# Moving the keys' turn behind the diagonal blocks, and two waits in steps of the weave, in a gated-delta decoder layer

## The chip, the cores and the metric

The kernel runs on one core of a Trainium2 chip. The metric is the device time of one execution in microseconds (us). The kernel before took 2161.29 us, the median of 3 runs between 2160.62 and 2162.14. Engines are TensorE (PE, matmuls), VectorE (DVE), ScalarE (ACT), GpSimd (POOL) and SyncE (SP); the last two, and ScalarE in a few places, also issue DMAs.

## The reference

One layer of a hybrid decoder, for one new sequence of 512 tokens and 8 sequences of one new token each (520 token columns), model width 2048, all in float32:

```python
h = h + W_out [ GatedDeltaNet(x_n) ; MultiScalePool(x_n) ],  where x_n = RMSNorm(h)
h = h + SwiGLU(RMSNorm(h))
```

One projection gives q, k, v, an output gate z, two gate logits and the pooling channels. q, k and v pass a causal convolution of 4 taps and SiLU. The delta group has 8 heads of width 128. Within a chunk of tokens a head solves a unit lower triangular system A U = V with A = I + (the strictly lower part of K K^T, scaled by beta and the decay), and between chunks it carries a 128 x 128 state:

```python
a_mat = m + jnp.eye(CHUNK, dtype=m.dtype)
u = lax.linalg.triangular_solve(a_mat, vc * bc[..., None], left_side=True,
                                lower=True, unit_diagonal=True)
...
v_new = u_i - jnp.einsum('bhck,bhkv->bhcv', w_i, S)
S = S * jnp.exp(g_last)[..., None, None] + jnp.einsum('bhck,bhcv->bhkv', k_dec, v_new)
```

The outputs are the two results of the layer, the final states, and the last rows for the convolution and the pooling.

## The kernel before, in words

**Products.** Each projection of 128 output columns (`product`) is 96 matmuls, 16 blocks of the inner dimension times two halves of the 520 columns times three: weights and activations are split into a high and a low part, and high x high, high x low and low x high are summed (lines 168 to 170, tile `mm`). The two halves hold a PSUM bank each, of three for all products, and are read out by VectorE (L259, `mixa<-mm` for the gate tiles z, `ext<-mm` for q, k and v); the product after next cannot start in a bank before that.

**The weave.** The small work of the heads is written as Python generators that lie between the matmuls of the products. After each 6 matmuls of a product `weave.step()` is called once; a step advances the first task of each of two tracks. A task that says `yield n` goes on n steps later, and `weave.add(task, track, delay)` starts one at least `delay` steps after the call. TensorE executes in the order in which the program was written, so a step count fixes where in the stream of matmuls a head's own matmuls (tile `dn`) stand. The other engines' streams are ordered by the framework's scheduler, which also goes by the order of the program, by what each instruction waits for and by its estimate of times; each of these streams then executes in that fixed order.

**Heads 0 to 3, then 4 to 7.** For each batch of four heads the products run k0 to k3, z0 to z3, then v and q of each head in turn. What the change touches:

- `turn_blocks` (L756 on) turns a 128 x 512 tile by 32 x 32 blocks. VectorE transposes into `bt` (L761 for keys and outputs, L766 for q and v), POOL stores that to memory (`tok_d`, L763 or L768) and loads it back with four DMAs (L771). For the keys the result is `kd`.
- `keys(h)` (L791 on, on track 1, 16 steps after its k product): the Gram matrix of the keys on TensorE (L795), its diagonal (L799, L801), a power -1/2 on POOL (L215, `rr`), scales `sck` (L805 to L808), the masked and scaled matrix (L810), then SyncE stores the 32 x 32 diagonal blocks (`nd_d`, L816) and POOL sets them to zero (L819).
- `eliminate(b)` (L823 on, track 1): SyncE loads the diagonal blocks of four heads (`nb<-nd_d`, L825). VectorE inverts all of them together by 31 pairs of instructions (L835, L837, tile `u`), copies the result transposed (L840, `ut`), and SyncE stores both (`ud_d`, L838 and L841).
- `qv_tiles(h)` (L1115 on): SyncE loads the inverted blocks into `utf` (L1117, four DMAs), the v product, v's taps (L737, L739, tile `y`), SiLU on ScalarE, v's turn into `vs`, then the same for q (`qT`, turned into `qk`); then `delta(h)` is added to track 0.
- `delta(h)` (L845 on): `xt_` from a product with the inverted blocks (L859), then the solution steps of a loop over `it` = 0, 1, 2 (matmul L869 into PSUM, VectorE L871 writes `uu`), each of which uses the `uu` of the step before, but the first. kd is scaled in step 0 (L874), vs in step 1 (L754). Then come four chunks, with the state `S` (L909, L911), and a tail that normalises the output (L931 to L936, a power on POOL among it) and turns it.

Loads of weights (`raw`, L131) stand on SyncE's queue among these DMAs; each is split into `hi` by ScalarE and `lo` by VectorE (L137).

Of the kernel before, what the change touches and what calls it, by code (L numbers as in the profile page):

```python
# [17 lines left out]
P = 128  # L18
# [3 lines left out]
SEQ = 512  # L22
# [47 lines left out]
def decoder_kernel(ctx, tc, x_prompt, x_sample, state_delta, state_conv, state_pool, norm_mix, w_in,  # L70
# [50 lines left out]
    weave = Weave()  # L121
# [399 lines left out]
    with ExitStack() as p1:  # L521
# [268 lines left out]
        def keys(h):  # L790
            kT, nn = mixb[:, h % 4, 0:SEQ], mixb[:, 4 + h % 4, 0:SEQ]  # L791
            _, dm = decay(h)
            gp_ = pst()
            for c in range(NCH):
                te.matmul(gp_[:, ck(c)], kT[:, ck(c)], kT[:, ck(c)], start=True, stop=True)  # L795
            ss = d1tile("ss", [P, NCH], "ss")
            junk = d1tile("junk", [P, P], "junk")
            for c in range(NCH):
                dve.scalar_tensor_tensor(junk, gp_[:, ck(c)], 1.0, ident, op0=ALU.mult, op1=ALU.mult,  # L799
                                         accum_out=ss[:, c:c + 1])  # L800
            dve.tensor_scalar(ss, ss, EPS, None, op0=ALU.add)  # L801
            rr = d1tile("rr", [P, NCH], "rr")
            pow_mhalf(rr, ss)
            fk, ik, ad = sck[:, h, 0, :], sck[:, h, 1, :], sck[:, h, 2, :]
            dve.tensor_tensor(fk, rr, rr, op=ALU.mult)  # L805
            dve.tensor_tensor(fk, fk, btok[:, 0:4, h], op=ALU.mult)
            dve.tensor_tensor(ik, ss, rr, op=ALU.mult)
            dve.tensor_tensor(ad, fk, edec[:, :, h], op=ALU.mult)  # L808
            for c in range(NCH):
                dve.scalar_tensor_tensor(nn[:, ck(c)], gp_[:, ck(c)], fk[:, c:c + 1], dm[:, ck(c)],  # L810
                                         op0=ALU.mult, op1=ALU.mult)
            yield 6 if h < 3 else 2
            nn3 = v3(nn)
            for q in range(4):
                r = slice(32 * q, 32 * q + 32)
                sp.dma_start(nd_d[h, q].rearrange("c s j -> s c j"), nn3[r, :, r])  # L816
            for q in range(4):
                r = slice(32 * q, 32 * q + 32)
                pool.memset(nn3[r, :, r], 0.0)  # L819


        def eliminate(b):
# [2 lines left out]
            sp.dma_start(nb.rearrange("p s j -> p (s j)"), nd_d[hs].rearrange("h q c s j -> (h q c) (s j)"))  # L825
            u = d1tile("u", [64, 32, 32], "u")
            uf = u.rearrange("p s j -> p (s j)")
            yield 10
            pool.memset(uf, 0.0)
            pool.memset(uf[:, 0:1024:33], 1.0)  # L830
            for t in range(31, 0, -1):
# [13 lines left out]
        def delta(h, qT, qk, vs):  # L845
# [19 lines left out]
            for it in range(3):  # L865
# [16 lines left out]
                                                 op0=ALU.mult, op1=ALU.mult)  # L882
                if it == 1:
                    scaled(vs, ik)
                yield 2

            op_ = pst()
            S = None
# [224 lines left out]
        def qv_tiles(h):  # L1113
            utf = utfs[h % 2].rearrange("p a c j -> p (a c) j")
            for q in range(4):  # L1115
                r = slice(32 * q, 32 * q + 32)
                sp.dma_start(utf[r, :, r], ud_d[h, q].rearrange("a c s j -> s (a c) j"))  # L1117
            vs = d1tile("vs", [P, SEQ], "vs")
            qkv_tile(2, h, vs)
            turn_blocks(2, h, vs, vs)  # L1120
            qT = d1tile("s0", [P, SEQ], "qT")
            qkv_tile(0, h, qT)
            qk = d1tile("tq", [P, SEQ], "qk")
            turn_blocks(0, h, qT, qk)
            weave.add(delta(h, qT, qk, vs), 0, 1)

        kds = {}
        for b in range(2):
            for h in range(4 * b, 4 * b + 4):
                qkv_tile(1, h, mixb[:, h % 4, 0:SEQ],  # L1130
                         {0: ext_first, 1: ext_second}.get(h))
                if h == 0:
                    weave.add(states())
                    weave.add(gates(), 1)
                kds[h] = d1tile("kd", [P, SEQ], "kd")
                turn_blocks(1, h, mixb[:, h % 4, 0:SEQ], kds[h])
                weave.add(keys(h), 1, 16)
            weave.add(eliminate(b), 1)
            for h in range(4 * b, 4 * b + 4):
# [966 lines left out]
```

## Time and profile before

| | before |
|---|---|
| median of 3 runs | 2161.29 us (2160.62 to 2162.14) |
| the profiled execution | 2161.12 us, span 2159.4 us |
| TensorE busy | 2127.0 us, 98% of the span |
| VectorE busy | 1772.2 us, 82% |
| ScalarE, POOL busy | 919.9 us (43%), 531.4 us (25%) |
| mean granted TensorE clock | 0.998 |

The span runs from the first to the last instruction of the profiled execution. A list of waits shows for each engine what ended its idle time: engine, line, releaser, total, number and longest. In a timeline a row is: start in us, duration in us, engine, line, operation, output and inputs, forms, number, and in square brackets the idle time before it with what ended it. A row of the windows gives a stretch in us, its length, then busy time and number of instructions of PE, PEld (weight loads), DVE, ACT and POOL, then the granted clock, the DMA share and GB/s.

### The profile page before, as it was taken

What the parts mean: (1) busy time and instruction counts of PE and PEld (TensorE: products, weight loads), DVE (VectorE), ACT (ScalarE), POOL (GpSimd) and SP (SyncE); (2) the same over time, 40 slices, a digit from 0 to 9 for tenths busy, and PEclk for the clock granted to TensorE, in tenths of its full rate; (3) what the DMA queues carried; (4) which work ended last, traced back from release to release, by engine and by line L of the source; (5) the groups of instructions that cost most, each with busy time, mean ns of one, the idle gap of its engine ahead of it and who ended that gap; (6) DMA issues with size and microseconds to landing.
All of it is one profiled execution on the core that took longest, in us unless ns stands there. A gap on an engine that the chain in (4) does not pass through costs nothing.

```text
span 2159.4 us, 43083 instructions
## 1 busy us (share of the span) xinstructions
PE 2127.0 (98%) x17681; PEld 2118.4 (98%) x17681; DVE 1772.2 (82%) x2715; ACT 919.9 (43%) x1340; POOL 531.4 (25%) x672
## 2 busy tenths in 40 slices
PE   8999999999999999999999999999999999999998
PEld 7999999999999999999999999999999999999998
DVE  7886677667599979988988988988877898887997
ACT  6433433343264544434434434434334444435444
POOL 2413441332012202233233233232113302003100
PEclk9999999999999999999999999999999999999999
DMA  8444454544445533554554454454456746438333
GB/s 281 126 125 118 130 141 122 132 125 126 122 118 162 156 114 115 150 167 141 144 164 144 143 168 142 142 169 133 121 147 189 233 112 205 115 104 248 91 108 119
DMA packets 449154, 313.84 MB, mean 145 GB/s; under 512 B 29116, under 2 KB 425813, under 8 KB 445613
## 3 DMA queue, kind: packets, MB, share of 16 engines
q1 hardware_dynamic: 422733, 219.94, 36.5%
q0 software_dynamic: 24912, 90.34, 13.4%
q8 instruction: 139, 2.28, 0.5%
q10 hardware_dynamic: 1312, 0.80, 0.1%
q14 instruction: 58, 0.48, 0.1%
HBM read 259.86 MB, written 51.82 MB: 144 GB/s over the span
## 4 chain that ended last, share of the span: by engine, by line
PE 82%; DVE 9%; DMA 3%; issue 2%; ACT 2%; POOL 1%; SPq 0%; DVEq 0%; ACTq 0%; POOLq 0%
PE dn L1252 21%; PE dn L1251 21%; PE dn L1253 21%; PE mm L168 5%; PE mm L169 5%; PE mm L170 5%; DVE lo L1245 1%; DMA vs<-tok_d 1%; DVE lo L137 1%; DVE y L739 1%; DMA st<-a_d 1%; DVE raw L1273 1%; PE dn L869 1%; DMA tok_d<-bt 1%; ACT hi L1244 0%
## 5 line engine op out<-in xcount | busy, mean ns | idle before, releaser
L1245 DVE TENSOR_TENSOR lo<-raw,hi 128x1024 fp32r<-128x1024 f32 (+1 forms) x422 | 527.9, 1271 | 89.0 <-ACT hi L1244 86.8
L1244 ACT CAST hi<-raw 128x1024 fp32r<-128x1024 f32 (+1 forms) x422 | 427.8, 1027 | 401.2 <-DVE raw L1273 195.5
L168 PE MATMUL mm<-xh,hi 128*128 128x256 f32 (+1 forms) x1280 | 380.3, 297 | 1.8 <-DVE mixa L259 1.8
L169 PE MATMUL mm<-xl,hi 128*128 128x256 f32 (+1 forms) x1280 | 362.1, 283 | 0.9 <-DVE xl L350 0.5
L170 PE MATMUL mm<-xh,lo 128*128 128x256 f32 (+1 forms) x1280 | 362.2, 283 | 0.4 <-DVE lo L137 0.4
L168 PEld LDWEIGHTS mm<-xh,hi 128*128 128x128 f32 x1280 | 242.1, 189 | 3.0 <-DVE mixa L259 2.2
L169 PEld LDWEIGHTS mm<-xl,hi 128*128 128x128 f32 x1280 | 242.3, 189 | 1.7 <-DVE xl L350 1.7
L170 PEld LDWEIGHTS mm<-xh,lo 128*128 128x128 f32 x1280 | 241.3, 189 | 0.6 <-DVE lo L137 0.6
L1252 PE MATMUL dn<-b21l,hi 128*128 128x260 f32 x620 | 175.8, 284 | 0.3 <-DVE b21l L1815 0.3
L1253 PE MATMUL dn<-b21h,lo 128*128 128x260 f32 x620 | 175.4, 283 | 0.0
L1251 PE MATMUL dn<-b21h,hi 128*128 128x260 f32 x620 | 175.0, 282 | 0.0
L1253 PE MATMUL dn<-b11h,lo 128*128 128x260 f32 x612 | 173.2, 283 | 1.3 <-DVE lo L1245 1.3
L1273 DVE TENSOR_TENSOR raw<-raw 128x1024 f32<-128x1024 f32 (+1 forms) x130 | 172.0, 1323 | 2.2
L1437 POOL TENSOR_TENSOR mixa<-mixa 128x520 f32<-128x520 f32 x22 | 50.2, 2280 | 501.6 <-DVE mixa L1431 501.6
L1252 PE MATMUL dn<-b11l,hi 128*128 128x260 f32 x612 | 173.3, 283 | 0.0
L1251 PE MATMUL dn<-b11h,hi 128*128 128x260 f32 x612 | 172.7, 282 | 0.0
L1251 PE MATMUL dn<-T1h,hi 128*128 128x260 f32 x556 | 158.1, 284 | 0.0
L1252 PE MATMUL dn<-T1l,hi 128*128 128x260 f32 x556 | 157.7, 284 | 0.0
L1253 PE MATMUL dn<-T1h,lo 128*128 128x260 f32 x556 | 156.7, 282 | 0.0
L1251 PE MATMUL dn<-B22h,hi 128*128 128x260 f32 x548 | 155.9, 284 | 0.0
L1252 PE MATMUL dn<-B22l,hi 128*128 128x260 f32 x548 | 155.6, 284 | 0.0
L1253 PE MATMUL dn<-B22h,lo 128*128 128x260 f32 x548 | 154.6, 282 | 0.4 <-DVE lo L1245 0.4
(664 smaller groups left out, 6552.6 us busy)
## 6 DMA issues: line engine op xcount, KB each, us to landing
raw<-in_w_gate_up_dram SPq DMA_DIRECT2D x134, 512.0 KB
raw<-in_w_in_dram SPq DMA_DIRECT2D x79, 512.0 KB
a_d<-mixa POOLq DMA_DIRECT2D x22, 1040.0 KB, 5.5
raw<-in_w_down_dram SPq DMA_DIRECT2D x48, 448.0 KB
mixb<-in_w_gate_up_dram SPq DMA_DIRECT2D x41, 512.0 KB
raw<-in_w_out_dram SPq DMA_DIRECT2D x25, 512.0 KB
st<-a_d POOLq DMA_DIRECT2D x49, 260.0 KB, 6.4
raw<-in_w_down_dram SPq DMA_DIRECT2D x24, 512.0 KB
```

Source lines behind the costliest of these rows:

```text
L137: dve.tensor_tensor(lo[:, r], raw[:, r], hi[:, r].bitcast(F32), op=ALU.subtract)
L168: te.matmul(acc[ci], wh, hi[k][:, c0:c1], start=(k == 0), stop=False)
L169: te.matmul(acc[ci], wh, lo[k][:, c0:c1], start=False, stop=False)
L170: te.matmul(acc[ci], wl, hi[k][:, c0:c1], start=False, stop=(k == len(w) - 1))
L739: dve.scalar_tensor_tensor(y, ext[:, i:i + SEQ], cw(i, t), y, op0=ALU.mult, op1=ALU.add)
L1244: act.copy(hi, raw)
L1245: dve.tensor_tensor(lo, raw, hi.bitcast(F32), op=ALU.subtract)
L1251: te.matmul(acc, wh[:, k, :], xf[:, k, :], start=start and k == 0, stop=False)
L1252: te.matmul(acc, wh[:, k, :], xg[:, k, :], start=False, stop=False)
L1253: te.matmul(acc, wl[:, k, :], xf[:, k, :], start=False, stop=stop and k == wh.shape[1] - 1)
L1273: dve.tensor_tensor(r[name], r[a], r[b], op=op)
L1437: pool.tensor_tensor(q[:, 4:8:2, :], q[:, 1:4:2, :], q[:, 0:2, :], op=ALU.subtract)
```

## The change

Three edits. The turn of a head's keys leaves the loop over the k products and is asked for later, in a new function `key_rows(h)`: for the first three heads of a batch one step after `keys(h)` has stored its diagonal blocks, for the fourth one step into `eliminate`. Head 0's `delta` is added with a delay of 5 steps instead of 1. In `delta` the wait after solution step 0 is 3 steps instead of 2. The later lines of the kernel move down by up to 9 (L859 becomes L868, L869 L878, L871 L880, L835 L844, L840 L849, L1117 L1126).

```diff
+            if h % 4 < 3:
+                yield 1
+                key_rows(h)
+
+        def key_rows(h):
+            kds[h] = d1tile("kd", [P, SEQ], "kd")
+            turn_blocks(1, h, mixb[:, h % 4, 0:SEQ], kds[h])
...
-            yield 10
+            yield 1
+            key_rows(4 * b + 3)
+            yield 9
             pool.memset(uf, 0.0)
...
                 if it == 1:
                     scaled(vs, ik)
-                yield 2
+                yield 3 if it == 0 else 2
...
-            weave.add(delta(h, qT, qk, vs), 0, 1)
+            weave.add(delta(h, qT, qk, vs), 0, 5 if h == 0 else 1)
...
-                kds[h] = d1tile("kd", [P, SEQ], "kd")
-                turn_blocks(1, h, mixb[:, h % 4, 0:SEQ], kds[h])
                 weave.add(keys(h), 1, 16)
```

The scheduler's order of the other engines moves with it. First place: VectorE near head 3's masked blocks (about 110 us). `mm_1362` and `mm_1363` before, `mm_1346` and `mm_1347` after, are the two halves of z1; `rr_1407` before and `rr_1417` after is head 3's power. Before:

```order
L259 TENSOR_TENSOR mixa_98<-mm_1362,rb_110 128x264
L799 SCALAR_TENSOR_TENSOR junk_1401,ss_1400<-dn_1395,ident_78 128x128
L874 TENSOR_TENSOR kd_969<-kd_969,sck_649 128x512
L799 SCALAR_TENSOR_TENSOR junk_1401,ss_1400<-dn_1395,ident_78 128x128
L259 TENSOR_TENSOR mixa_98<-mm_1363,rb_110 128x256
L801 TENSOR_SCALAR ss_1400<-ss_1400 128x4
L805 TENSOR_TENSOR sck_649<-rr_1407 128x4
L807 TENSOR_TENSOR sck_649<-ss_1400,rr_1407 128x4
L806 TENSOR_TENSOR sck_649<-sck_649,btok_635 128x4
L808 TENSOR_TENSOR sck_649<-sck_649,edec_633 128x4
L810 SCALAR_TENSOR_TENSOR mixb_99<-dn_1395,sck_649,dm_1389 128x128 x4
```

After:

```order
L805 TENSOR_TENSOR sck_649<-rr_1417 128x4
L807 TENSOR_TENSOR sck_649<-ss_1410,rr_1417 128x4
L779 SCALAR_TENSOR_TENSOR dm_2167<-gcb_2165,gcs_631,mneg_89 128x128
L259 TENSOR_TENSOR mixa_98<-mm_1346,rb_110 128x264
L806 TENSOR_TENSOR sck_649<-sck_649,btok_635 128x4
L779 SCALAR_TENSOR_TENSOR dm_2167<-gcb_2165,gcs_631,mneg_89 128x128
L808 TENSOR_TENSOR sck_649<-sck_649,edec_633 128x4
L810 SCALAR_TENSOR_TENSOR mixb_99<-dn_1405,sck_649,dm_1399 128x128 x2
L259 TENSOR_TENSOR mixa_98<-mm_1347,rb_110 128x256
L810 SCALAR_TENSOR_TENSOR mixb_99<-dn_1405,sck_649,dm_1399 128x128 x2
```

Both evictions of z1 now stand behind the first use of head 3's power, and one of them between the masked blocks.

Second place: VectorE at the end of the first elimination (about 155 us), where `bt_1967` is the transpose for v of head 0. Before:

```order
L835 TENSOR_TENSOR tm_1588<-nb_1437,u_1439 64x87
L766 STREAM_TRANSPOSE bt_1967<-vs_1844 128x4x4x32
L837 TENSOR_TENSOR u_1439<-u_1439,tm_1588 64x3x29
L835 TENSOR_TENSOR tm_1591<-nb_1437,u_1439 64x60
L837 TENSOR_TENSOR u_1439<-u_1439,tm_1591 64x2x30
L835 TENSOR_TENSOR tm_1594<-nb_1437,u_1439 64x31
L837 TENSOR_TENSOR u_1439<-u_1439,tm_1594 64x31
L840 COPY ut_1598<-u_1439 64x1024
```

After:

```order
L739 SCALAR_TENSOR_TENSOR y_1960<-ext_1845,prm_103,y_1960 128x512
L844 TENSOR_TENSOR tm_1605<-nb_1447,u_1449 64x31
L739 SCALAR_TENSOR_TENSOR y_1960<-ext_1845,prm_103,y_1960 128x512
L846 TENSOR_TENSOR u_1449<-u_1449,tm_1605 64x31
L849 COPY ut_1609<-u_1449 64x1024
L766 STREAM_TRANSPOSE bt_1967<-vs_1844 128x4x4x32
```

The transpose moved from ahead of the last three pairs to behind the copy.

Third place: VectorE in the solution steps of head 2, where `y_2887` are the taps of q of head 2. Before:

```order
L754 TENSOR_TENSOR vs_2507<-vs_2507,sck_649 128x512
L739 SCALAR_TENSOR_TENSOR y_2887<-ext_2713,prm_103,y_2887 128x512 x3
L871 SCALAR_TENSOR_TENSOR uu_2956<-dn_2970,utf0_645 96x4x96
L766 STREAM_TRANSPOSE bt_2895<-qT_2712 128x4x4x32
L853 TENSOR_TENSOR qts_2947<-qT_2712,gcb_2938 128x512
L871 SCALAR_TENSOR_TENSOR uu_2956<-dn_2989,utf0_645 96x4x64
```

After:

```order
L754 TENSOR_TENSOR vs_2507<-vs_2507,sck_649 128x512
L739 SCALAR_TENSOR_TENSOR y_2887<-ext_2707,prm_103,y_2887 128x512 x2
L880 SCALAR_TENSOR_TENSOR uu_2956<-dn_2970,utf0_645 96x4x96
L739 SCALAR_TENSOR_TENSOR y_2887<-ext_2707,prm_103,y_2887 128x512
L766 STREAM_TRANSPOSE bt_2895<-qT_2706 128x4x4x32
L862 TENSOR_TENSOR qts_2947<-qT_2706,gcb_2938 128x512
L880 SCALAR_TENSOR_TENSOR uu_2956<-dn_2995,utf0_645 96x4x64
```

One of q's three taps moved behind the first `uu`.

## The prediction

> **What bounds the kernel now.** I read the page first, then the waits of TensorE, then the clock by windows, then the timelines of the engines around the largest wait.
>
> ```profile
> span 2159.4 us, 43083 instructions
> PE 2127.0 (98%) x17681; PEld 2118.4 (98%) x17681; DVE 1772.2 (82%) x2715; ACT 919.9 (43%) x1340; POOL 531.4 (25%) x672
> ```
>
> TensorE is busy for 98% of the span, so only its 32 us of idle time, and time at a lower clock, can be won without changing the matmuls; the edits change none. The waits of TensorE say where the idle time lies:
>
> ```profile
> PE dn L859 <- DMA utf<-ud_d: 4.5, 1, 4.5
> PE dn L409 <- DMA pr<-in_norm_mix_dram: 4.0, 1, 4.0
> ...
> PE dn L869 <- DVE uu L871: 3.1, 6, 0.6
> ...
> PE mm L168 <- DVE mixa L259: 1.8, 1, 1.8
> PE dn L894 <- DVE S L909: 1.6, 1, 1.6
> ```
>
> (Columns: total us, times, longest.) The edits can reach four of these: head 0's L859 waits once for the solved triangles, six second solution steps (L869) wait 0.3 to 0.6 each for the step before, one product waits 1.8 for its PSUM bank, and head 3's first state waits 1.6. The largest has a second cost, in the granted clock (the 1.00 or so ahead of the DMA share):
>
> ```profile
> 0.00:20.00 20.00, 11.96 (x72) 10.98 (x73) 12.71 (x32) 11.41 (x25) 4.44 (x18) 1.00 0.96 321
> 20.00:160.00 140.00, 135.56 (x1113) 131.96 (x1112) 113.74 (x325) 61.67 (x94) 44.72 (x78) 1.00 0.56 156
> 160.00:180.00 20.00, 16.20 (x121) 16.23 (x122) 10.11 (x23) 6.16 (x15) 5.82 (x12) 0.83 0.49 123
> 180.00:2160.00 1980.00, 1963.26 (x16379) 1959.21 (x16377) 1635.67 (x2338) 840.68 (x1206) 476.43 (x565) 1.00 0.50 143
> ```
> ```profile
> 162.00:163.00 1.00, 0.00 (x0) 0.00 (x0) 0.00 (x0) 0.00 (x0) 0.00 (x0) 0.81 0.82 161
> 163.00:164.00 1.00, 0.20 (x1) 0.23 (x2) 0.99 (x2) 0.00 (x0) 0.00 (x0) 0.50 1.10 324
> ...
> 169.00:170.00 1.00, 1.00 (x10) 1.00 (x10) 0.25 (x1) 0.99 (x2) 0.53 (x1) 0.78 0.21 33
> ```
> ```profile
> 163.80 1.99 PE L859 MATMUL dn<-utf,mixb 128*128 128x96 f32 x8 [4.53 <-DMA utf<-ud_d]
> ...
> 170.94 0.81 PE L869 MATMUL dn<-uu,xt__2157 128*96 128x64 f32 x8
> ```
>
> The idle time begins at 163.80 - 4.53 = 159.27. The clock halves at 162.6 (0.81 = 1 - 0.38 x 0.5) and is whole again at 169.44 (0.78 = 1 - 0.44 x 0.5). The matmuls from 163.80 to 169.44 thus lose 5.64 / 2 = 2.8 us: this one wait costs 4.5 + 2.8 = 7.3 us. No other wait shows a dip, not even the 4.0 us at the start.
>
> **What ends that wait.** The rows of VectorE, POOL and SyncE before it:
>
> ```profile
> 123.59 0.20 DVE L835 TENSOR_TENSOR tm<-nb,u 64x31 f32<-64x31 f32 x1 [3.88 <-DMA nb<-nd_d]
> ...
> 153.43 0.71 DVE L766 STREAM_TRANSPOSE bt<-vs 128x512 f32<-128x512 f32 x1
> ...
> 155.22 1.12 DVE L840 COPY ut<-u 64x1024 f32<-64x1024 f32 x1
> ...
> 163.01 0.69 DVE L754 TENSOR_TENSOR vs<-vs,sck 128x512 f32<-128x512 f32 x1 [2.48 <-DMA vs<-tok_d]
> 163.62 1.53 DVE L739 SCALAR_TENSOR_TENSOR y<-ext,prm,y 128x512 f32<-128x512 f32 x2
> ...
> 167.17 1.81 DVE L779 SCALAR_TENSOR_TENSOR dm<-gcb,gcs,mneg 128x128 f32<-128x128 f32 x4
> 169.75 0.55 DVE L871 SCALAR_TENSOR_TENSOR uu<-dn,utf 96x384 f32<-96x384 f32 x1 [0.77 <-issue]
> ```
> ```profile
> 113.58 1.26 SPq L816 DMA_DIRECT2D nd_d<-mixb  x3
> 114.94 0.39 SPq L131 DMA_DIRECT2D raw<-in_w_in_dram  x1
> 115.37 2.04 SPq L816 DMA_DIRECT2D nd_d<-mixb  x1
> ...
> 119.89 0.54 SPq L825 DMA_DIRECT2D nb<-nd_d  x1
> ```
> ```profile
> 115.12 0.20 POOL L819 MEMSET mixb<- 32x128 f32 x1 [2.73 <-DMA nd_d<-mixb]
> ...
> 154.44 0.62 POOL L768 DMA_DIRECT2D tok_d<-bt  x1 [1.48 <-DVE u L837]
> 157.35 2.18 POOL L771 DMA_DIRECT2D vs<-tok_d  x4 [2.29 <-issue]
> ```
>
> The diagonal blocks go to memory, come back at 123.59, the elimination takes VectorE until 155.22 (31.6 us, other heads' work mixed in), and its result passes through memory to L859 at 163.80. Call the start of the copy of u E; before, E = 155.22, and the triangles are there 163.80 - 155.22 = 8.6 us behind E. A second chain ends nearly as late: v's turn lands at 163.01, and uu of head 0's first step (L871) stands on VectorE behind L754, two taps, a transpose, qts and four L779: from 163.01 it could start at 163.01 + 5.97 = 168.98 and end 6.5 us behind the landing.
>
> **The change part by part.**
>
> *The delay of 4 steps and the additional step.* A weave step is 6 matmuls of 0.1195 us, 0.72 us. Head 0's L859 comes 24 matmuls later (2.9 us), its second solution step 30 (3.6 us). No work is added; products that came behind come ahead. So if the second step starts at the same time as before (170.94), TensorE is 30 x 0.1195 = 3.58 us ahead. That is the gain to be had, whatever waits stand before it, as long as TensorE then still waits for uu; what counts is when uu is ready.
>
> *The key turn behind the diagonal blocks.* It takes no instruction away; five DMA issues per head (one tok_d, four kd) and one transpose move. On VectorE the order at the end of the elimination moves v's transpose behind the copy (order above). From the rows: copy at E, transpose ends E + 1.04 + 0.65 = E + 1.7; before it ended at 154.14 and v landed 8.9 us later, so v lands at E + 10.6, and uu ends at E + 17.1. (The memset of u that now stands between v's store and its loads on POOL is 0.97 us within the 2.9 us that the loads waited anyway; bare, it would cost 1.0.)
>
> E itself goes by the head 3 blocks. Two evictions of z1's product now stand behind head 3's rr power on VectorE (order above), and on POOL head 1's power now comes ahead of three of head 3's kd loads, head 2's still behind them.
>
> ```profile
> 110.26 0.42 DVE L259 TENSOR_TENSOR mixa<-mm,rb 128x256 f32<-128x256 f32 x1
> ...
> 111.94 0.16 DVE L805 TENSOR_TENSOR sck<-rr 128x4 f32<-128x4 f32 x1 [1.19 <-POOL rr L215]
> ...
> 112.42 1.12 DVE L810 SCALAR_TENSOR_TENSOR mixb<-dn,sck,dm 128x128 f32<-128x128 f32 x4
> ```
> ```profile
> 110.42 0.28 PE L168 MATMUL mm<-xh,hi 128*128 128x256 f32 x1
> ```
>
> One after another by the rows of before, the instructions that now stand ahead of head 3's masked blocks (L810) end them at 114.5 instead of 113.5. Of their four stores, 0.42 us of issue each, the last was issued behind a weight load and landed 119.89 - 115.37 = 4.5 us later; the first, without one, 115.12 - 113.58 = 1.5 later. Now the four are issued together, the last at 115.8: it lands at 117.3 to 120.3, and with the 3.7 us of the read (119.89 to 123.59) the elimination starts at 121.0 to 124.0. It keeps its length of 155.22 - 123.59 = 31.6 less the transpose (0.6) plus one eviction more (0.4), 31.4. E = 152.4 to 155.4; I take 154.2, nearer the late end, since other weight loads are under way. Then uu ends at 171.3, TensorE starts its second step 0.1 later at 171.4, and the gain is 3.58 - (171.4 - 170.94) = **3.1 us** (1.9 to 4.9 by the ends).
>
> Where the idle time then lies: z2's second chunk, due at 110.42, gets its bank when z1's eviction ends, now at some 112.7 (2.3 us; 1.5 to 3.3); the triangles land at E + 8.6 = 162.8, while L859 is due at 159.27 - 1.8 (bank wait gone) + 2.3 + 2.9 = 162.7: a wait near 0. The second step is due 30 matmuls (3.6 us) and two sets of solution matmuls (at whole clock some 1.5, half of what the rows above show at the half one) later, at 167.9, and waits 3.5 us. 2.3 + 0.1 + 3.5 = 5.9 stands against 9.1 before (4.5 + 2.8 + 1.8): the same 3.2 us, if no clock dip comes.
>
> *The additional step in heads 1 to 7.* The wait to win is 3.1 us in six heads. Heads 2, 3, 5, 6: VectorE is late because its work for the head before is in its way.
>
> ```profile
> 231.38 2.32 DVE L739 SCALAR_TENSOR_TENSOR y<-ext,prm,y 128x512 f32<-128x512 f32 x3
> 233.61 0.55 DVE L871 SCALAR_TENSOR_TENSOR uu<-dn,utf 96x384 f32<-96x384 f32 x1
> ```
>
> The head before ends one step later as well, so the distance to the second step is unchanged; but one tap (0.77) now stands behind uu (order above), so the first uu ends 0.7 earlier, which covers the wait of 0.57. The tap, q's SiLU, the transpose and qts (0.77 + 0.63 + 0.71 + 0.65) then stand ahead of the second uu, which ends about 0.6 after the third step is due. The stall goes one step on: 0 for each of the four (0.6 if it doesn't: 2.3 in all; a loss of 0.3 at the other end). Head 1 wins its 0.5, since head 0's tail is cleared before its uu. Head 3's state copy waited 1.6 because a decay term late by a DMA, a low part and a gate stood ahead of it on VectorE; one of them now stands behind, so 1.0 (0 to 1.6). Together **1.5 us** (0 to 4.4). Heads 4 to 7's triangles end no wait in the list: nothing there.
>
> Sum: 3.1 + 1.5 = 4.6 us off 2161.12 (the profiled execution, 1.7 us more than its span, 0.2 under the median): **2156.5 us**.
>
> **The rivals.**
>
> *All idle time gathers at one place.* If z2 doesn't wait for a bank (VectorE reaches z1's eviction earlier), TensorE comes to the second step at 165.6, waits 5.8 us there, and the clock halves again: a loss of 2.8. Gain 3.1 - 2.8 + 1.5 = 1.8: 2159.3. For it: the one wait of 4.5 did this, 3.3 us in, and my own 3.5 is near. Against it: the wait of 4.0 at the start did not, and the eviction's place behind the power is fixed by the order. The Trainium skill, page "TensorE: Matmul & The Clock Gate", section "Part 1: The HAM clock gate", says that the clock halves after a wholly idle window of 3.4 us, and that the windows run freely; the 6.8 us between the two turns here are two such windows. By it a wait of 3.5 us would halve the clock in few cases, (3.5 - 3.41) / 3.41 of them as an estimate, and one of 5.8 us in seven of ten.
>
> *Everything hides.* The chain to E runs 3 us or more earlier (powers no longer behind kd loads): all of 7.3 + 1.8 + 3.1 + 1.6 = 13.8 could go, 2147.3; half of it is likelier, 2151 to 2153. Against it: uu's place behind v's turn.
>
> *Nothing moves in truth.* The order puts the transposes and turns of heads 0 to 2 where they were; the wait for triangles becomes a wait for uu of the same end, with E late by 2 (157): 3.58 - 3.3 = 0.3, and the heads' stalls each move one step on: 2160.8.
>
> *Slower.* With uu at E + 17.2, the gain at head 0 is 157.3 - E. If head 3's power comes 1.5 us later than I have it (POOL runs its three kd loads ahead of one power, and VectorE waits for each), L810 ends at 116.0, the last store lands the slow way at 121.8, the read ends at 125.5, and E = 156.7 to 157. Then L859 waits again, 162.7 to 165.5, the second step 170.6 to 174.2, and each is near the idle time that halves the clock: 0.3 - 2.8 for one dip, and nothing from the heads: 2163.6. It decides from E = 156 on, if a dip comes with it.
>
> **How the numbers follow.** Forecast 0.55, gathered idle 0.12, everything hides 0.10, nothing 0.13, slower 0.10. About 0.2% (4.3 us) is what a measurement of this kernel tells from no change, so the line is at 2157.0, close to the forecast: of its 0.55 I count 0.34 as faster and 0.21 as same. Faster 0.34 + 0.10 = 0.44; same 0.21 + 0.12 + 0.13 = 0.46; slower 0.10. The forecast's own range, 1.9 + 0 to 4.9 + 4.4 us off, is 2151.8 to 2159.2; taking in the gathered idle, nothing and the half of what hides gives 2151.5 to 2162.0.
>
> **What would show it.** Right: no wait of over 1 us for utf<-ud_d, granted clock 1.00 from 160 to 180, a wait of 2 to 4 us at head 0's second solution step for uu, one of 1.5 to 3.3 at a product near 110 us for mixa L259, and the copy of u at 153 to 155. The six waits of the second steps should turn into waits of the third. Wrong: the copy at 157 or later, a second dip of the clock, or a wait of over 1 us in the heads that the waits of before don't list.

## The result and the profile after

The change is **slower**: 2173.31 us, the median of 6 runs (2171.29 to 2175.73), against 2161.27 for the kernel before, also of 6 runs beside them (2160.62 to 2163.54). The ratio is 1.0054, its 95% interval 1.0041 to 1.0067: 12 us lost where 4.6 were forecast as won. The profiled execution took 2171.29 us, the least of the six, 10.2 over that of the kernel before; the traces speak for these 10.2.

The page and TensorE's list of waits (total us, times, longest):

```profile
span 2169.6 us, 43068 instructions
...
PE 2131.8 (98%) x17681; PEld 2120.2 (98%) x17681; DVE 1773.6 (82%) x2715; ACT 919.8 (42%) x1340; POOL 533.2 (25%) x672
```
```profile
PE mm L168 <- DVE mixa L259: 5.8, 3, 3.4
...
PE dn L878 <- DVE uu L880: 4.1, 7, 1.2
PE dn L878 <- ACT xt__2181 L870: 4.1, 1, 4.1
```

The wait for the triangles (4.5 before) is gone as forecast. In its place stand one of 4.1 for a copy on ScalarE, and a wait for PSUM banks that rose from 1.8 to 5.8. TensorE's timeline tells where (in brackets the idle time):

```profile
112.58 0.38 PE L168 MATMUL mm<-xh,hi 128*128 128x256 f32 x1 [2.00 <-DVE mixa L259]
...
170.94 0.77 PE L878 MATMUL dn<-utf,xt__2181 128*96 128x96 f32 x4 [4.11 <-ACT xt__2181 L870]
...
175.43 0.81 PE L878 MATMUL dn<-uu,xt__2181 128*96 128x64 f32 x8
...
361.85 0.38 PE L168 MATMUL mm<-xh,hi 128*128 128x256 f32 x1 [3.40 <-DVE mixa L259]
```

They are the z2 product, head 0's *first* solution step, and a z product of the second batch. Each is followed by a dip of the clock (here the stretches ahead of the three dips, and one microsecond within each; columns as before, the clock ahead of the DMA share):

```profile
160.00:180.00 20.00, 15.89 (x127) 15.69 (x126) 10.79 (x20) 5.21 (x7) 6.50 (x14) 0.91 0.50 119
...
114.00:115.00 1.00, 1.00 (x7) 1.00 (x6) 0.90 (x3) 1.00 (x2) 0.00 (x0) 0.50 0.00 0
...
173.00:174.00 1.00, 1.00 (x7) 1.00 (x6) 1.00 (x4) 0.28 (x1) 0.00 (x0) 0.50 0.56 168
...
363.00:364.00 1.00, 1.00 (x6) 1.00 (x6) 1.00 (x4) 0.60 (x2) 0.00 (x0) 0.50 0.40 117
...
109.73:113.14 3.41, 1.41 (x12) 1.21 (x11) 2.48 (x15) 0.42 (x1) 1.60 (x4) 1.00 0.59 155
167.77:171.18 3.41, 0.24 (x2) 0.24 (x3) 2.68 (x4) 1.27 (x3) 0.10 (x1) 1.00 0.01 1
358.89:362.30 3.41, 0.45 (x3) 0.46 (x4) 3.31 (x8) 0.48 (x2) 0.00 (x0) 1.00 0.20 50
```

Each dip lasts 3.4 us and costs half of that, 1.7.

**What ends these waits.** SyncE, VectorE, ScalarE and POOL in the changed kernel:

```profile
114.33 1.73 SPq L816 DMA_DIRECT2D nd_d<-mixb  x4
116.10 0.43 SPq L776 DMA_DIRECT2D gcb<-gcr_d  x1
117.07 0.40 SPq L131 DMA_DIRECT2D raw<-in_w_in_dram  x1
117.66 0.54 SPq L832 DMA_DIRECT2D nb<-nd_d  x1
122.00 0.39 SPq L131 DMA_DIRECT2D raw<-in_w_in_dram  x1
```
```profile
112.10 0.43 DVE L259 TENSOR_TENSOR mixa<-mm,rb 128x264 f32<-128x264 f32 x1
...
123.55 0.20 DVE L844 TENSOR_TENSOR tm<-nb,u 64x31 f32<-64x31 f32 x1 [1.58 <-DMA nb<-nd_d]
...
154.97 1.15 DVE L849 COPY ut<-u 64x1024 f32<-64x1024 f32 x1
156.02 0.72 DVE L766 STREAM_TRANSPOSE bt<-vs 128x512 f32<-128x512 f32 x1
...
167.72 0.69 DVE L754 TENSOR_TENSOR vs<-vs,sck 128x512 f32<-128x512 f32 x1 [4.97 <-DMA vs<-tok_d]
168.33 1.53 DVE L739 SCALAR_TENSOR_TENSOR y<-ext,prm,y 128x512 f32<-128x512 f32 x2
...
340.34 0.16 DVE L805 TENSOR_TENSOR sck<-rr 128x4 f32<-128x4 f32 x1 [3.58 <-POOL rr L215]
...
351.12 0.20 DVE L844 TENSOR_TENSOR tm<-nb,u 64x31 f32<-64x31 f32 x1 [4.18 <-DMA nb<-nd_d]
...
361.37 0.42 DVE L259 TENSOR_TENSOR mixa<-mm,rb 128x264 f32<-128x264 f32 x1
```
```profile
169.89 0.63 ACT L740 ACTIVATE qT<-y 128x512 f32<-128x512 f32 x1 [9.06 <-DVE y L739]
170.43 0.46 ACT L870 COPY xt__2181<-dn 128x384 f32<-128x384 f32 x1
```
```profile
161.21 2.18 POOL L771 DMA_DIRECT2D vs<-tok_d  x4 [2.27 <-ACT hi L135]
...
338.59 0.67 POOL L771 DMA_DIRECT2D kd<-tok_d  x1 [2.77 <-issue]
339.28 1.03 POOL L215 TENSOR_TENSOR rr<-ss,mhalf 128x4 f32<-128x4 f32 x1
```

First batch: head 3's four stores are issued together and land by 117.2, where POOL's last memset behind them starts (119.9 before). The read of the blocks is issued 2.2 us earlier than before (117.66 against 119.89), but 0.6 us behind a weight load, and takes 5.9 us (to 123.55) instead of 3.7: the elimination starts no earlier. (Before, a load was issued during the read too, but 0.65 us behind it, at 120.54.) Its copy of u begins at 154.97; v's turn lands at 167.72, VectorE holds two taps behind it, q's SiLU on ScalarE (169.89) waits for those, and the copy `xt` that the first solution step needs stands behind that SiLU.

Second batch: POOL runs the last head's power (339.28) behind a kd load, ahead of which POOL was idle for 2.77 us. The scales wait 3.58 for it, and the elimination starts at 351.12. Before:

```profile
334.56 0.17 DVE L805 TENSOR_TENSOR sck<-rr 128x4 f32<-128x4 f32 x1 [1.22 <-POOL rr L215]
...
343.98 0.20 DVE L835 TENSOR_TENSOR tm<-nb,u 64x31 f32<-64x31 f32 x1 [1.23 <-DMA nb<-nd_d]
```

That is 7.1 us later, 4.6 more than the 2.5 by which TensorE is late there. The reading out of a z product stands behind the twelfth pair of the elimination on VectorE in both kernels (361.37 in the change), so the product waits 3.40 for its bank.

**A ledger.** The traces of all these kernels hold the same 4,264 product matmuls (tile `mm`) in the same order, so the start of the n-th of them can be compared. The table gives how many us later it starts than before, in the profiled executions of the change and of the experiments below. The first three columns lie ahead of head 0's solution, the fourth between the two batches, the fifth behind the second batch's bank wait and its dip, the last behind the last head; at all of them the same other work has been done. What a row shows at 107 arose at the start of that execution.

| product matmul at (us, before) | 107 | 114 | 152 | 343 | 358 | 594 |
|---|---|---|---|---|---|---|
| the change | 0.0 | 3.8 | 2.4 | 2.5 | 8.4 | 10.5 |
| turn alone (e1) | 0.0 | 2.3 | 4.2 | 7.5 | 8.7 | 9.8 |
| delay alone (e2) | 0.4 | 0.4 | -0.1 | -2.0 | -2.0 | -2.2 |
| step alone (e3) | 0.1 | 0.1 | -0.3 | -0.4 | -0.4 | 2.3 |
| delay and step (e4) | 0.3 | 0.3 | 0.2 | -4.1 | -4.1 | -1.4 |
| change, late turn in batch 1 only (e5) | 0.2 | 3.9 | 2.4 | 1.8 | 2.2 | 5.2 |
| change, late turn in batch 2 only (e6) | 0.4 | 0.4 | 0.1 | -3.1 | 2.5 | 4.7 |
| change, two weight loads left out (e17) | 0.0 | 3.8 | 1.5 | -3.3 | 2.2 | 4.3 |
| delay and step, the same loads left out (e18) | -0.1 | -0.1 | -1.0 | -1.3 | -0.6 | 2.2 |

### The profile page after: what moved, and what is told of

Same layout as the page of the kernel before. It is cut to its first block, busy times and chain, and to the rows that moved or that the text cites. A ratio compares the mean times of both kernels' runs of the same rounds, so it can differ in the third digit from the quotient of the medians.

```text
span 2169.6 us, 43068 instructions
## 1 busy us (share of the span) xinstructions
PE 2131.8 (98%) x17681; PEld 2120.2 (98%) x17681; DVE 1773.6 (82%) x2715; ACT 919.8 (42%) x1340; POOL 533.2 (25%) x672
## 4 chain that ended last, share of the span: by engine, by line
PE 75%; DVE 6%; issue 2%; DMA 2%; ACT 1%; POOL 1%; SPq 0%; DVEq 0%; ACTq 0%; POOLq 0%
PE dn L1258 21%; PE dn L1259 21%; PE dn L1260 21%; PE mm L168 3%; PE mm L170 2%; PE mm L169 2%; DVE lo L1252 1%; DVE raw L1280 1%; DVE lo L137 1%; DMA tok_d<-bt 1%; PE mm L1258 0%; DMA nd_d<-mixb 0%; PE mm L1259 0%; PE mm L1260 0%; PE dn L993 0%
```

## The experiments

The main theory, A in the texts on record, is that the late turn itself costs the time, by what it does to the other engines' order. The rivals are that the delay or the step does it, and others as they came up. All were run beside the kernel before; the ratios are to that.

### Each edit alone: e1 to e4

The turn alone is the first two hunks of the change and the last. The others, on the kernel before:

```diff
-            weave.add(delta(h, qT, qk, vs), 0, 1)
+            weave.add(delta(h, qT, qk, vs), 0, 5 if h == 0 else 1)   # e2, e4
-                yield 2
+                yield 3 if it == 0 else 2                            # e3, e4
```

> Only the key turn is moved; both waits in steps are as before. Theory A (the loss is the key turn's: in the second batch it puts head 7's power behind a kd load on POOL, the elimination starts some 5 us later, TensorE waits 3.4 us for a bank there and the clock halves after it): 2167 to 2172 us, with a wait of about 3 us for mixa L259 near 360 us and one of about 2 near 112. Rival B (the loss is the additional step's) and rival C (it is head 0's delay): 2160 to 2163, no such waits.

> Only head 0's delta rule starts 4 steps later. Theory A: 24 matmuls (2.9 us) go ahead of L859, so its wait falls from 4.5 to some 1.7 us and the clock stays whole (2.8), while about 1 us of waiting comes at the second solution step: 2156 to 2158. Rival B: the same. Rival C (the idle time gathers behind ScalarE's copy xt or at uu, over 3 us, and the clock halves there): 2161 to 2165.

> Only the additional step between the first two solution steps. Theory A: the waits go from the second step to the third, head 0 stays as it was: 2160 to 2162.5. Rival B (the tail of each head and the next head's steps come nearer to one another, new waits in heads 1 and 7): 2165 or more. Rival C: as theory A.

> The change without the key turn. Theory A: about the delay alone, 0 to 1 us under it, 2155 to 2158, so the turn's share of the whole is 15 us or more. Rival B: 2163 or more. Rival C: 2161 to 2165.

| | median us | ratio, interval |
|---|---|---|
| e1 turn alone | 2167.99 | 1.0032, 1.0019 to 1.0044 |
| e2 delay alone | 2158.09 | 0.9992, 0.9984 to 1.0001 |
| e3 step alone | 2162.21 | 1.0013, 1.0004 to 1.0022 |
| e4 delay and step | 2160.40 | 1.0001, 0.9992 to 1.0010 |

The turn alone makes it slower, as A has it, though not at the place that A named: near 360 us it waits only 0.90 for a bank, and most is lost in the first batch (2.98 us for z3's bank, 1.86 at the first triangle product, 2.23 at the first use of uu, and behind the last two 3.4 and 10.2 us at half clock). Its five runs lie between 2162.94 and 2169.57, and the one in the ledger is the slowest. The delay alone is at the best a small gain. Delay and step together stand above the 2155 to 2158 that A had for them. The step alone moves the waits of 0.5 from the second to the third steps and wins nothing: by the ledger it costs 2.7 us between 358 and 594, in heads 4 to 7. There the order on VectorE is another as well. In head 4 the update of the state behind the second chunk (L911) came ahead of two taps and the low part of a weight, and ended 1.5 us before the third chunk needed it; in e3 it stands behind them, and TensorE waits:

```profile
407.95 0.33 DVE L911 SCALAR_TENSOR_TENSOR S<-S,egl,dn 128x128 f32<-128x128 f32 x1
```
```profile
408.34 0.49 PE L894 MATMUL dn<-S,mixb 128*128 128x128 f32 x2 [0.29 <-DVE S L911]
```

In each of heads 4 to 7 the third chunk's matmul with the state (L894), and in the last head the fourth's too, starts some 0.055 us behind the end of such an update. These five start 0.28 to 0.57 us behind the matmul ahead of them instead of 0.12, and the matmul behind each follows 0.21 us later instead of 0.11: 1.8 us in all. Only 0.45 of it is in the list of waits; most of the rest counts as busy, because the recorded 0.28 us of the matmul ahead cover it.

### One batch's late turn at a time: e5 and e6

```diff
-            if h % 4 < 3:
+            if h % 4 < 3 and h // 4 == 0:          # e6: == 1
...
-            key_rows(4 * b + 3)
+            if b == 0:                             # e6: == 1
+                key_rows(4 * b + 3)
...
+                if b != 0:                         # e6: != 1
+                    key_rows(h)
```

> The change, but heads 4 to 7 turn their keys in the old place; only heads 0 to 3 turn them late. Theory A (the late turn costs in both batches: z1's eviction behind head 3's power in the first, head 7's power behind a kd load in the second): some 4 us over the change without the turn, 2163 to 2166; the wait near 112 us for mixa L259 stays at 2.0, the wait of 3.4 near 360 is gone. Rival D (only the second batch costs, since the elimination of the first starts at 123.55 as before): 2159 to 2162.

> The change, but heads 0 to 3 turn their keys in the old place; only heads 4 to 7 turn them late. Theory A: 5 to 6 us over the change without the turn, 2164 to 2168, with the elimination of the second batch about 5 us late against TensorE, a wait of 2.5 to 3.5 us for mixa L259 near 350 and mostly a clock dip behind it. Rival D: 2169 to 2173.

Late in batch 1 only: 2165.82 us, 1.0024 (1.0014 to 1.0034). Late in batch 2 only: 2165.68, 1.0023 (1.0014 to 1.0033). Each batch's late turn costs about half of the loss. In the first kernel the waits of 1.89 (z2) and 3.74 (`xt`) are there, and none near 360; in the second it is the other way round. Its list of waits:

```profile
PE mm L168 <- DVE mixa L259: 5.0, 3, 3.1
...
PE dn L869 <- DMA utf<-ud_d: 1.8, 1, 1.8
```

The two add up: 0.0024 + 0.0023 - 0.0001 (e4, which both contain) = 0.0046, within the change's 0.0041 to 0.0067. The ledger says the same: the late turn costs 5.6 to 5.9 us up to 343 (2.5 against -3.1; 1.8 against -4.1) and about 5.5 between 343 and 358.

### Is it the engine that issues the turn, the delay, or the banks? e7 to e11

```diff
+            eng = act if kind == 1 else pool
-                pool.dma_start(d.rearrange("c p f -> p c f"), v3(bt))
+                eng.dma_start(d.rearrange("c p f -> p c f"), v3(bt))
...
-            weave.add(delta(h, qT, qk, vs), 0, 5 if h == 0 else 1)
+            weave.add(delta(h, qT, qk, vs), 0, 9 if h == 0 else 1)
...
-    ps_mm = ctx.enter_context(tc.tile_pool(name="ps_mm", bufs=3, space=PSUM))
-    ps_dn = ctx.enter_context(tc.tile_pool(name="ps_dn", bufs=5, space=PSUM))
+    ps_mm = ctx.enter_context(tc.tile_pool(name="ps_mm", bufs=4, space=PSUM))
+    ps_dn = ctx.enter_context(tc.tile_pool(name="ps_dn", bufs=4, space=PSUM))
```

The first piece (with the same for the loads) is e7, the second e8, both on the change; the third is e9 on the change, e10 on the kernel before, e11 on the delay alone.

> The change, with the five DMAs of each key turn issued by ScalarE instead of POOL, so that no power stands behind a kd load on POOL. Theory A: head 7's power comes about 2.5 us earlier against TensorE, the wait of 3.4 near 360 falls to about 1 and the clock stays whole there; in the first batch 1 us: 2166 to 2170, more if ScalarE's casts are held up by the loads. Rival H (VectorE's own order, the late transpose and the scaling of kd ahead of the elimination, delays it, not POOL): no change, 2172 to 2174.

> The change with a delay of 9 steps for head 0 instead of 5. Theory A (head 0's first solution step waits until 170.9 us for ScalarE's copy xt, which stands behind q's SiLU and so behind v's turn): 24 matmuls or 2.9 us more go ahead of it, its wait of 4.1 falls to about 1.2 and the clock stays whole: 2168 to 2170. Rival F (head 0's tail comes nearer to head 1's steps, which then wait by as much): 2172 to 2174.

> The change with four PSUM banks for the products (mm) and four for the small work (dn) instead of three and five. Theory A (what the late turn costs comes through the products' banks: late evictions on VectorE stall z products, and the later v product then makes v's turn and head 0's copy xt late): the waits of 2.0 near 112 and 3.4 near 360 us go, head 0's first solution step waits 1 to 2 us less, and two or three clock dips go: 2161 to 2165, near its own control e10. Rival I (the heads' small work pays for the bank it lost): 2172 or more, with new waits at dn. Rival D2 (the late elimination itself costs, whatever the banks): 2170 to 2173.

> The kernel before with four and four banks, the control for e9 and e11. Theory A: only the wait of 1.8 near 135 us goes, and L859 then waits that much longer: 2159 to 2162. Rival I: 2164 or more, with waits at dn in the heads.

> The delay of head 0 alone, with four and four banks. Theory A: 2156 to 2159, as the delay alone, since the bank wait of 1.3 near 135 only moves into the wait for the triangles. Rival I: 2162 or more.

| | median us | ratio, interval |
|---|---|---|
| e7 keys' turn issued by ScalarE | 2174.67 | 1.0065, 1.0053 to 1.0078 |
| e8 change with delay 9 | 2174.10 | 1.0063, 1.0049 to 1.0077 |
| e9 change, four banks for products | 2177.41 | 1.0080, 1.0063 to 1.0097 |
| e10 before, four banks | 2162.23 | 1.0010, 1.0001 to 1.0019 |
| e11 delay alone, four banks | 2162.40 | 1.0010, 1.0000 to 1.0019 |

None helps, and e7 to e9 show the same thing. With ScalarE issuing the turn, VectorE waits only 1.19 for the last head's power in batch 2 instead of 3.58, and the bank wait of 3.4 becomes 1.31 and 1.38: A's mechanism is there. But a state copy then waits 2.64 and z3 3.28. With a delay of 9 the first solution step waits 1.1 instead of 4.1, but z3's bank 3.13. With four banks the bank waits are gone, but the triangles wait 4.06, `xt` 3.02 and uu of head 4 5.15. So the bank waits are only where lateness comes out first. That it is the elimination's lateness for which TensorE pays at each of these other places is argued from this, not shown. Four banks by themselves cost 1.9 us (e10), and the delay alone 4.3 more with them than with three (e11 against e2), which A did not have.

### The changed kernel again, and who issues the read: e12 to e15

```diff
-            sp.dma_start(nb.rearrange("p s j -> p (s j)"), nd_d[hs].rearrange("h q c s j -> (h q c) (s j)"))
+            pool.dma_start(nb.rearrange("p s j -> p (s j)"), nd_d[hs].rearrange("h q c s j -> (h q c) (s j)"))
```

e12 is the change with no edit. e13 has this edit on the change, e14 on the delay alone; e15 is e14 with the stores of the blocks (L816) issued by POOL too.

> The change as it is, profiled once more. Theory G (the clock is judged in windows of 3.41 us that run freely, so a wait of 2 to 4 us halves it or not by where it falls): the waits come out within 0.2 us of the first profile, but the dips begin at other places or are more or fewer, by 1.7 us each; the time within 2170 to 2176. Rival J (each wait has its own fixed result for the clock): dips again at 113, 171 and 362 us only.

> The change, with the read of the diagonal blocks (nb) issued by POOL instead of SyncE, so that it is not queued behind the weight load issued 0.6 us ahead. Theory K (the slow read breaks what VectorE's order counts on): the read takes 4 to 5 us instead of 5.9 to 7.9, the elimination of the first batch starts at 121.5 to 122.5, z3 does not wait, v's turn lands 1 to 3 us earlier: 2168 to 2171, from some 2172.5. Rival L (the weight load takes the DMA engines whichever queue the read is in): start at 123.5 to 125.5 and no change.

> Head 0's delay alone, with the read of the blocks issued by POOL: the control. Theory K: there the read took 3.9 us behind the last store, with no load ahead of it, so it gains nothing, 0 to 1 us lost to POOL's issue: 2158 to 2160. Rival L: the same.

> Head 0's delay alone, with the stores of the diagonal blocks and their read issued by POOL, so that neither stands among SyncE's weight loads. Theory K: the last store of head 3 lands up to 2.5 us earlier than the 119.6 of the delay alone, the elimination starts at 121 to 122.5, L859 waits under 1 us and the clock stays whole: 2154 to 2158. Rival M (POOL's stores hold up its powers and memsets, and the elimination starts no earlier): 2159 to 2163.

e12, a single execution, took 2169.93 us. The same instructions in the same order wait elsewhere than in the other profile of the change. SyncE, and VectorE's first pair:

```profile
117.46 0.53 SPq L832 DMA_DIRECT2D nb<-nd_d  x1
120.29 0.39 SPq L131 DMA_DIRECT2D raw<-in_w_in_dram  x1
```
```profile
125.35 0.20 DVE L844 TENSOR_TENSOR tm<-nb,u 64x31 f32<-64x31 f32 x1 [5.09 <-DMA nb<-nd_d]
```

Here the second weight load was issued 2.8 us behind the read (4.3 in the first profile, at 122.00), and the read took 7.9 us; z3's bank then waited 3.06, the first solution step 2.40. That two executions would agree within 0.2 us, as the text had it, was wrong.

The first batch's read in all the traces bears the weight loads out. It took 3.5 to 3.9 us in the eight whose nearest load was issued 0.6 us behind it (the kernel before, e2, e3, e4, e6, e10, e11, e16); 5.8 and 5.9 with one 0.6 ahead and the next 4.3 behind (e5, the change); 6.4 to 8.1 with one 0.6 to 1.1 ahead and the next 1.1 to 2.8 behind (e9, e1, e8, e12, e7). All slow ones have a load issued shortly *ahead* of the read.

With the read on POOL's queue (e13) it was issued at 116.77 and came at 124.78, 8.0 us, with a weight load of SyncE 0.4 us ahead of it and another 3.0 behind; the time was 2174.54 (1.0064, 1.0051 to 1.0077). e14 took 2165.02 (1.0020, 1.0012 to 1.0029), e15 2163.95 (1.0015, 1.0006 to 1.0024), both more than the delay alone. In e14 the read took only 4.2 us (a load 1.3 ahead, the next 8 behind); it loses at a bank wait of 1.84 and at the triangles, 3.74, with 10.2 us at half clock behind the two, and why was not followed. In e15 the last store and the read are issued later, and the elimination starts at 126.12. So the queue isn't what holds the read. By the Trainium skill, page "DMA: Bandwidth & Descriptors", section "Issuing engines are not separate DMA queues", issuing from several engines saves only the time of issue, since the transfers share the same DMA engines; e13 agrees, with 8.0 us on the other queue.

### The delay of 9 without the turn: e16

The second piece above, on the kernel before, whose delay was 1.

> The kernel before with a delay of 9 steps for head 0 and nothing else. Theory A: L859's wait of 1.9 goes, uu is ready when the second step comes, no dip, and head 1's steps wait 1 to 2 us longer behind head 0's tail: 2155.5 to 2158.5. Rival F (all that is won at head 0 is waited for in head 1): 2158.5 to 2161.

2160.01 us, 0.9999 (0.9990 to 1.0008). The triangles' wait and every dip are gone, but the first solution step waits 3.31 for `xt`, a state copy 2.45 and head 1 1.50. More delay only moves the wait on.

### The weight loads beside the read taken away: e17 and e18

```diff
...
-                load()
+                if i in (16, 17):
+                    pool.memset(raw[:, :f], 0.01)
+                else:
+                    load()
```

`i` numbers the weight loads; e17 is on the change, e18 on delay and step without the turn. Two halves of weight blocks of head 0 are left out.

> The change, with two weight loads left out: those of the second half of head 0's v product and the first half of its q product, which are filled with a constant by POOL instead, so the outputs that hang on them are not the reference's. VectorE's order keeps every eviction and tap at the same pair. Theory K (the weight loads beside it make the read of the blocks take 5.9 to 8 us, which breaks what VectorE's order counts on): the read takes 3 to 4 us, the elimination of the first batch starts at 121 to 122, z3 does not wait, v's turn lands 2 to 3 us earlier than 167.7: 2167.5 to 2170.5. Rival N (the order alone, more pairs ahead of the evictions, makes the waits): the same waits, 2171.5 to 2174.5.

> The delay and the step without the late turn, with the same two weight loads left out (filled with a constant, so the outputs that hang on them are not the reference's). Theory K: the four stores of head 3 go together, the last lands near 117, the read takes 3 to 4 us and the elimination starts at 120.5 to 122 instead of 123.7; L859's wait of 1.7 falls under 0.5: 2157.5 to 2160. Rival N: 2160 to 2162, with z3 waiting longer.

e17 took 2166.59 us (1.0036, 1.0022 to 1.0049), 6.3 us over the kernel before of its runs (2160.34) where the change is 12.0 over, with the instructions of VectorE around the elimination in the same order. Its SyncE, VectorE, and windows:

```profile
114.34 1.73 SPq L823 DMA_DIRECT2D nd_d<-mixb  x4
116.12 0.43 SPq L783 DMA_DIRECT2D gcb<-gcr_d  x1
117.26 0.53 SPq L839 DMA_DIRECT2D nb<-nd_d  x1
```
```profile
120.76 1.23 DVE L141 TENSOR_TENSOR lo<-raw,hi 128x1024 fp32r<-128x1024 f32 x1 [4.32 <-DMA nb<-nd_d]
121.90 0.20 DVE L851 TENSOR_TENSOR tm<-nb,u 64x31 f32<-64x31 f32 x1
...
163.02 0.69 DVE L761 TENSOR_TENSOR vs<-vs,sck 128x512 f32<-128x512 f32 x1 [1.10 <-DMA vs<-tok_d]
```
```profile
160.00:180.00 20.00, 19.71 (x170) 19.21 (x169) 15.23 (x30) 7.28 (x18) 6.30 (x16) 1.00 0.50 130
```

Without the loads the read takes 3.5 us (117.26 to 120.76), v's turn lands at 163.02 instead of 167.72, the first solution step waits 0.25 instead of 4.1, and the clock stays whole from 160 to 180. In that the trace is like the picture of the prediction, with the turn in its new place. Not all of it is the read's: the copy of u comes 1.7 us earlier (153.30), v's turn 4.7, because it now takes 9.7 us from that copy on instead of 12.75. Most of these 3.0 lie between the issue of its four loads and their landing (4.0 us instead of 6.5). There too a weight load stands nearer in the change (162.12, 0.9 us behind the first of the four; 161.28, 2.3 us behind, in e17), but no run separates that. By the ledger e17 stands 3.3 us ahead of the kernel before at 343, about as e6 does (3.1), whose first batch has the early turn; the change is 2.5 behind. The second batch, whose loads were left in, loses 5.5 us, as in the change and e6. What stays in batch 1 is z2's wait, 2.04 and its dip.

e18 took more than theory K had: 2162.97 (1.0013, 1.0004 to 1.0022), no better than e4. Its read took 3.2 us (117.99 to 121.23), but VectorE's order is another there, and `xt` waited 2.96 with a dip behind it. So leaving out these loads doesn't help by itself; it takes away the harm of the late turn in batch 1.

## Why the prediction was wrong

*What bounds the kernel, and the gain to be had in heads 0 to 3: right in size, in part by luck.* Delay and step without the turn put TensorE 4.1 us ahead at the end of the first batch (e4). The prediction had 3.1 for head 0, 0.5 for head 1 and 1.0 for head 3: 4.6, but for the three edits together. Head 1's wait didn't go (0.50 before, 0.89 in e4, 1.15 in the change). The wait for the triangles fell from 4.53 to 1.74, in the change to nothing, and the waits of the second steps of heads 2, 3, 5 and 6 became waits of 0.50 to 0.53 at the third.

*The read of the blocks: wrong, and with it most of batch 1.* "With the 3.7 us of the read" was a duration from a read that had no weight load issued just ahead. The stores landed at 117.2, the early end of the forecast range; in the new order the read then ran behind a load and took 5.9 us, or 7.9 where the next load came sooner. The elimination started at 123.55 in one profile and 125.35 in the other (forecast 121.0 to 124.0), took the forecast 31.4 us in the first, and E with 154.97 was in its range; but what the stores won was used up. That the loads do it is shown by e17, which takes them away (3.5 us), and by the traces in which they lie otherwise.

*v's landing: wrong by 2.1 us.* It was put at E + 10.6 and came at E + 12.75 (167.72). POOL issued its four loads 4.2 us behind the store (157.03 to 161.21) instead of 2.9, which makes 1.3 of it; the rest is the transfer, 6.5 us instead of 5.7.

*Which step waits: wrong.* The prediction followed VectorE's queue from v's landing to uu and found the second step late. It left out ScalarE's: `xt` of the first step stands behind q's SiLU there, and that behind the two taps that follow v's landing on VectorE. So the first step waits, 4.11, and the second comes at 175.43 and not at 171.4.

*z2's bank wait: its length right, its price not.* Forecast 2.3 (1.5 to 3.3), measured 2.00. The dip of 1.7 behind it was not in the sum: in the kernel before only the largest wait had shown one. The ledger's 3.8 at 114 is the two together. That z1's evictions behind head 3's power cause it is told by the rows (the eviction at 112.10 ends at 112.53, z2 goes on at 112.58), not by a run; e17 still has it. And that the wait of 4.0 us at the start showed no dip, which the prediction held against one here, can't be told from the windows' 1.00 alone: the sixteen transposes right behind it (L334, 7.14 us) took 3.77 us, 0.24 each, where four at 15.34 us took 0.60, 0.15 each, which looks like a low clock.

*"Heads 4 to 7's triangles end no wait in the list: nothing there": wrong, the largest single miss.* The wait of 3.40 and its dip stand in the second batch, 5.9 us in the ledger. The prediction looked at POOL's order in the first batch only. That an instruction ended no wait in the kernel before doesn't mean that it has room: the z evictions were interleaved with the elimination's pairs at fixed places, and a start 4.6 us later was enough. e5 and e6 show it.

*The additional step in heads 4 to 7: wrong sign.* Forecast between 0 and a small gain; from 358 to 594 the ledger has a loss of 2.1 to 3.0 us in each of its kernels with the step, of 1.1 with the turn alone, and a gain of 0.2 with the delay alone. In the last head the stall doesn't move on but comes twice, 0.37 and 0.53. The prediction followed uu alone and left out the state: of the 2.7 us of e3 the five matmuls that came late for the state are 1.8 and the last head's additional stall 0.6; some 0.3 stay open.

The sum by its measured terms: -4.1 (delay and step, heads 0 to 3) + 5.9 (late turn, batch 1) + 5.5 (late turn, batch 2) + 2.7 (step, heads 4 to 7) = 10.0, against 10.5 in the ledger and 10.2 between the two spans. Of the "slower" rival the mechanism (a late last store, E late by 2 us, one dip) was not what happened: the store was in time, in the first profile E too, and there were three dips. In e12 the read ended at 125.35 and E was 156.75, the rival's figures, but through the length of the read.

Open stay e14's loss, e18's late `xt`, the longer transfer of v's turn, and why two executions of the change issue the second weight load 1.7 us apart. No run beat the kernel before by more than can be told from no change; the delay alone, 0.9992 (0.9984 to 1.0001), came nearest.

## What to carry to other kernels

A small DMA on the critical chain is to be costed by what else is issued around it in the *new* order: its duration here went from 3.2 to 8.1 us with weight loads issued shortly ahead of it, whichever queue it was on. Where streams are fixed in order ahead of the run, a move is to be followed through every place where it applies (each batch) and on every queue of the chain (ScalarE's here), not only where the largest wait stood. A wait that is moved is not won: four kernels here (e7, e8, e9, e16) removed or shortened it at one place and paid at the next.

## What was not expected of the hardware

*Waits of 2 us can halve the clock.* The dips of one execution lie on a grid: in the change they begin at 113.14, 171.18 and 362.30, which are 17.0 and 56.0 times the length of one dip, 3.413 us, apart. The stretch of the grid ahead of a dip needn't be idle altogether. The delay alone has a single wait of 1.86 us, and half a clock in the 3.4 us behind it; e12 has one of 3.14 without a dip, which lies on two stretches of its grid (first the stretch ahead of the delay's dip, then three of e12):

```profile
160.67:164.08 3.41, 1.55 (x13) 1.38 (x12) 0.88 (x2) 0.00 (x0) 0.00 (x0) 1.00 1.07 250
```
```profile
356.75:360.16 3.41, 2.08 (x18) 1.87 (x16) 3.20 (x8) 0.00 (x0) 0.00 (x0) 1.00 0.28 84
360.16:363.58 3.42, 1.61 (x13) 1.61 (x14) 3.28 (x10) 1.45 (x3) 0.00 (x0) 1.00 0.55 153
124.67:128.08 3.41, 0.85 (x7) 0.85 (x8) 2.45 (x11) 0.42 (x1) 0.00 (x0) 1.00 0.05 12
```

TensorE was busy 1.55 of 3.41 us (45%) ahead of the delay's dip, 0.85 (25%) ahead of the one in e12, and 1.41 (41%), 0.24 and 0.45 ahead of the three in the change. In e12 the stretches with 2.08 and 1.61 (61% and 47%) had none behind them. So a wait costs by how it lies on the grid: a stretch busy for less than about half is followed by a half clock. Laid over all 20 traces, the grid has 39 stretches at whole clock in which TensorE was busy for less than 45%, and a half clock follows every one; none follows where it was busy for 50% or more; of the seven between, four have one. The way back is less clear. In the turn alone (e1) the clock fell behind a stretch busy 1.38 of 3.41, and then stayed half for two stretches more, though the rows have TensorE busy for 3.21 and 3.42:

```profile
170.23:173.64 3.41, 1.38 (x12) 1.18 (x10) 2.68 (x5) 1.91 (x2) 0.70 (x3) 1.00 0.00 0
173.64:177.05 3.41, 3.21 (x17) 3.21 (x18) 1.95 (x6) 1.15 (x2) 1.95 (x4) 0.50 0.43 113
177.05:180.47 3.42, 3.42 (x19) 3.42 (x19) 0.29 (x1) 0.00 (x0) 0.81 (x2) 0.50 0.25 75
180.47:183.88 3.41, 3.41 (x19) 3.41 (x17) 1.63 (x5) 1.05 (x1) 0.00 (x0) 0.50 0.11 31
```

That is how a wait of 2.23 cost another 5.1. What counts as busy there is open. The Trainium skill, page "TensorE: Matmul & The Clock Gate", section "Part 1: The HAM clock gate (the "warmup" mystery)", has the windows run freely at 3413 ns, and the clock fall after an idle one. The grid agrees with the first; the measured 45% contradicts the second, by which none of the waits of 2 us could have halved the clock, and the measurement decides.

*A read's time varies between executions of one kernel by 2 us* (5.9 and 7.9 in the two profiles of the change), where a load on SyncE's queue is issued 1.7 us apart, and with it the place where TensorE waits.
